# Gate columns z, the gate and the state-space part of the output projection: a move ahead of and into the third attention pattern

## The chip, the core and the metric

One of the eight cores of a Trainium2 chip runs the whole layer. The metric is the device time of one execution in microseconds; a set of runs is told by its median. The core's engines are TensorE (PE in the rows, its weight loads PEld), VectorE (DVE), ScalarE (ACT), GpSimd (POOL) and SyncE (SP), whose only work here is to issue DMAs. The order of the instructions on each engine is fixed when the program is built, and each engine, SyncE's queue of DMAs too, goes through its own in that order.

## What is computed

A one-layer decoder trunk over 1024 prompt rows and 8 decode rows, T = 1032 columns in the kernel (activations lie transposed: features on partitions, rows as columns). The mixer, cut to what matters:

```
qkv, z, xbc, dt = split(rmsnorm(x) @ w_in)
for g in 3 patterns:                         # windows 128, 512, 2048; dilations 1, 4, 16
    o[g], lse[g] = dilated_window(rope(q[g]), rope(k[g]), v[g])
attn = sum(softmax(lse over g)[g] * o[g])    # "merge", (.., 512)
y    = ssd_chunked(conv(xbc), dt)            # (.., 1024)
ssm  = rmsnorm((y + d_skip * xs) * silu(z), ssd_norm_w)
mix  = concat(attn, ssm) @ w_out
x    = x + rmsnorm(mix); x = x + rmsnorm(swiglu(rmsnorm(x)))
```

The decode rows attend over caches of past keys and values with the same weights.

## The kernel before

All is float32. Operands of the large products are split into two exact parts (`xh`, `xl` for the input; `wh`, `wl` for a weight tile), and a product is the sum of three: xh·wh, xh·wl, xl·wh. `load_w` loads a 128x1024 weight tile (L141) and GpSimd splits it (L156, L158). `unit` (L169) multiplies one tile with one of three chunks of 344 columns: 8 steps of 128 by 3 parts, 24 matmuls. `gemm` does so for its chunks, and `scaled` (L239) evicts each from PSUM by VectorE, times the row scale.

A scheduler of the Tile framework sets each engine's order by priority: the kinds are "evac", "w" (weights), "side", "late" and "main", in falling rank. The large matmuls are "main" and stand in the order in which the program is written; attention, gate and merge steps go in between where their inputs come.

The stages in the order of the program: xBC columns, convolution and state-space scan (its output goes to DRAM, `y_d`); `pattern(0)`, `pattern(1)`, `pattern(2)`, each with four head pairs; per pair `do_v`, `do_qk` twice (rotation: ScalarE L614, GpSimd L615, VectorE L619) and `attend`, eight blocks of scores, softmax and values (L645 to L687), whose result goes to `n_d` (L689). `dec_scores(g)` (L747 to L754) follows each pattern: keys of the caches times a broadcast query (GpSimd L748, VectorE L749). Behind `pattern(2)` come the rest of the decode scores, then:

- the merge, of "late" rank: the three patterns' statistics come back from DRAM (`sn`, L818), give weights (`w_d`, L844); then 16 steps, four quarters of 256 columns by four head pairs, each: load of three patterns' rows `nt` (L849) and of the weights `wt` (L852), GpSimd multiply (L854), VectorE adds (L855, L856), ScalarE cast to `ah` (L857), VectorE rest to `al` (L858). The pool `mgp` holds two `nt` and two `wt`.
- the values of the caches, "late" too: 24 loads `cvt` (L870) through five buffers, GpSimd and VectorE multiplies (L873), VectorE adds (L876, L877), a matmul (L878) each for eight rows.
- z columns and gate, 8 gemms: eviction to `zt` (L239), load of `y_d` (L907), silu (L909), multiply to `yg` (L910), squares (L913, L915), their sum `acc` on GpSimd (L917); then the norm's weights split the gated rows into `sh` and `sl` (L923, L924), in buffers that held `xh` and `xl`; and `rt`, the row scale (L192).
- state-space part of the output projection: chunks 0 and 1 of eight output tiles, 48 matmuls each, into `mix`; the first two tiles side by side, step by step as `sh` and `sl` come (L954).
- attention part: `load_pair` (L976 to L979) casts on ScalarE and splits on GpSimd, `unit` with `ah` and `al` (12 matmuls a chunk), added to `mix` (L1010); chunk 2 of the state-space part stands between; norms, and SwiGLU.

## Time and profile before

| | us |
|---|---|
| median of 3 runs (lowest, highest) | 1947.85 (1947.51, 1948.57) |
| span of the profiled execution | 1955.3 |
| TensorE busy in it | 1827.1 (93%) |
| VectorE busy | 1071.0 (55%) |
| GpSimd busy | 856.4 (44%) |
| ScalarE busy | 549.2 (28%) |

The times of single instructions come from the profiled execution, whose span is the figure that they add up to. TensorE is busy for 93% of it, but the share is an average over stages; of the 40 slices of the span the ones from the 21st on, behind the third pattern, fall to 7 and 8 tenths, and the granted clock falls to 8 tenths there.

### The profile page before, as it was taken

The numbers are of one execution on the slowest core, as the hardware profiler recorded it, in microseconds if no ns is written. First come the engines' busy times: TensorE is split into PE (matmuls) and PEld (weight loads), VectorE is DVE, ScalarE is ACT, GpSimd is POOL, SyncE is SP. The second block draws the span as 40 slices with busy tenths as digits, with TensorE's granted clock in tenths as the row PEclk, the third lists the DMA queues.
The fourth block names the chain that finished last, engine by engine and source line by source line (L and its number), as shares of the span: only waits on it lengthen the run. The fifth ranks groups of instructions, "written<-read, shape, count | busy, mean of one in ns | idle before, by whom it ended". The sixth has DMA issues, their size and how long they took to land.

```text
span 1955.3 us, 29265 instructions
## 1 busy us (share of the span) xinstructions
PE 1827.1 (93%) x11685; PEld 1712.4 (88%) x11685; DVE 1071.0 (55%) x1917; ACT 549.2 (28%) x1084; POOL 856.4 (44%) x557
## 2 busy tenths in 40 slices
PE   7999989999999999998789889999999999999994
PEld 7998777888887898886678879999999999999993
DVE  7866776768774554556884796330233223321348
ACT  5322344343533344452231334111111001100142
POOL 6332356665435534356755564223223332233325
PEclk9999999999999999999889999999999999999997
DMA  5322333443324433365554444236533753355362
GB/s 188 114 92 87 111 110 100 126 127 110 117 83 153 161 99 104 130 233 150 154 158 130 134 134 151 97 128 244 178 108 103 253 172 119 119 202 196 116 251 87
DMA packets 125545, 275.27 MB, mean 141 GB/s; under 512 B 17616, under 2 KB 83632, under 8 KB 124000
## 3 DMA queue, kind: packets, MB, share of 16 engines
q1 hardware_dynamic: 125408, 273.39, 42.8%
q8 instruction: 92, 1.51, 0.3%
q14 instruction: 45, 0.37, 0.1%
HBM read 235.86 MB, written 125.47 MB: 185 GB/s over the span
## 4 chain that ended last, share of the span: by engine, by line
PE 39%; DVE 7%; DMA 2%; issue 1%; POOL 1%; ACT 1%; DVEq 0%; SPq 0%; POOLq 0%; ACTq 0%
PE g L169 14%; PE pu L169 12%; PE pg L169 12%; DMA nt<-n_d 1%; DVE mix L1030 1%; DVE fl L1033 1%; PE g L954 1%; DVE nt L856 1%; DVE nt L855 1%; DMA xr<-in_xT 0%; DVE mix L1029 0%; POOL nt L854 0%; DVE fr L192 0%; DVE nr L192 0%; DVE sl L924 0%
## 5 line engine op out<-in xcount | busy, mean ns | idle before, releaser
L169 PE MATMUL g<-xh,wh 128*128 128x344 f32 x1344 | 446.0, 332 | 32.4 <-DVE rw L239 12.7
L169 PE MATMUL g<-xl,wh 128*128 128x344 f32 x1344 | 443.2, 330 | 2.8 <-DVE xl L218 2.7
L169 PE MATMUL g<-xh,wl 128*128 128x344 f32 x1344 | 441.9, 329 | 1.9 <-POOL wl L158 1.2
L156 POOL TENSOR_SCALAR wh<-wr 128x1024 fp32r<-128x1024 f32 (+1 forms) x133 | 140.4, 1056 | 674.5 <-PE g L169 355.8
L158 POOL TENSOR_TENSOR wl<-wr,wh 128x1024 fp32r<-128x1024 f32 (+1 forms) x133 | 312.8, 2352 | 9.8
L169 PEld LDWEIGHTS g<-xh,wh 128*128 128x128 f32 x1344 | 258.1, 192 | 46.4 <-issue 14.4
L169 PEld LDWEIGHTS g<-xh,wl 128*128 128x128 f32 x1344 | 258.1, 192 | 11.5 <-issue 7.5
L169 PEld LDWEIGHTS g<-xl,wh 128*128 128x128 f32 x1344 | 258.0, 192 | 11.0 <-issue 6.1
L239 DVE TENSOR_TENSOR u<-pu,rf 128x344 f32<-128x344 f32 x66 | 34.0, 515 | 237.5 <-PE pu L169 237.5
L169 PE MATMUL pg<-fh,wh 128*128 128x344 f32 x504 | 158.8, 323 | 4.9 <-DVE mix L1010 4.9
L169 PE MATMUL pg<-fl,wh 128*128 128x344 f32 x504 | 162.1, 322 | 0.0
L169 PE MATMUL pu<-fl,wh 128*128 128x344 f32 x504 | 161.8, 321 | 0.0
L169 PE MATMUL pg<-fh,wl 128*128 128x344 f32 x504 | 161.4, 320 | 0.0
L169 PE MATMUL pu<-fh,wh 128*128 128x344 f32 x504 | 161.0, 319 | 0.0
L169 PE MATMUL pu<-fh,wl 128*128 128x344 f32 x504 | 160.4, 318 | 0.0
L169 PE MATMUL g<-hl,wh 128*128 128x344 f32 x432 | 137.8, 319 | 0.0
L169 PE MATMUL g<-hh,wl 128*128 128x344 f32 x432 | 137.4, 318 | 0.0
L169 PE MATMUL g<-hh,wh 128*128 128x344 f32 x432 | 137.1, 320 | 0.0
L659 ACT ACTIVATE sm<-sm,ngm 128x128 f32<-128x128 f32 (+1 forms) x192 | 84.9, 443 | 183.5 <-DVE ngm L655 177.2
L1088 ACT CAST hh<-s 128x344 fp32r<-128x344 f32 x66 | 31.7, 480 | 296.6 <-DVE s L1087 296.6
L614 ACT COPY sw<-rw 32x1032 f32<-32x1032 f32 x96 | 101.0, 1052 | 30.5 <-DVE rw L239 29.4
L1085 ACT ACTIVATE s<-s 128x344 f32<-128x344 f32 x66 | 32.5, 492 | 247.6 <-DVE s L239 247.4
(325 smaller groups left out, 3815.9 us busy)
## 6 DMA issues: line engine op xcount, KB each, us to landing
out_skv<-in_cache SPq DMA_DIRECT2D x64, 1023.5 KB, 5.4
wr<-in_w_in SPq DMA_DIRECT2D x56, 512.0 KB, 3.7
wr<-in_w_fin SPq DMA_DIRECT2D x44, 512.0 KB, 3.6
out_skv<-in_cache SPq DMA_DIRECT2D x16, 1022.0 KB, 5.4
wr<-in_w_out SPq DMA_DIRECT2D x24, 512.0 KB, 4.7
wr<-in_w_fout SPq DMA_DIRECT2D x24, 384.0 KB, 3.9
e<-cs_d SPq DMA_DIRECT2D x16, 512.0 KB, 4.1
n_d<-nh SPq DMA_DIRECT2D x12, 512.0 KB, 3.6
```

The source lines that it names most:

```text
L156: nc.gpsimd.tensor_scalar(out=wh[:, :cols], in0=wr[:, :cols], scalar1=1.0, scalar2=0.0, op0=ALU.mult, op1=ALU.add)
L158: nc.gpsimd.tensor_tensor(out=wl[:, :cols], in0=wr[:, :cols], in1=wh[:, :cols], op=ALU.subtract)
L169: nc.tensor.matmul(ps, x[:, ws], y[:, c0:c1], start=(k == 0 and j == 0), stop=(k == n - 1 and j == 2))
L239: return nc.vector.tensor_tensor(out=dst, in0=ps, in1=r[:dst.shape[0], c0:c1], op=ALU.mult)
L614: nc.scalar.copy(sw[q * 32:(q + 1) * 32, 0:T], rw[s * 32:(s + 1) * 32, :])
L659: nc.scalar.activation(out=sm[:, h, :nk], in_=sm[:, h, :nk], func=AF.Exp, scale=SCALE, bias=ngm[:, g, j, i:i + 1], accum_out=den[:, g, j, ...
L855: nc.vector.tensor_tensor(out=nt[:, 0], in0=nt[:, 0], in1=nt[:, 1], op=ALU.add)
L856: nc.vector.tensor_tensor(out=nt[:, 0], in0=nt[:, 0], in1=nt[:, 2], op=ALU.add)
L954: nc.tensor.matmul(pq[m][c], ws[m][j == 1][:, k * P:(k + 1) * P], (sl if j == 2 else sh)[k][:, CH[c][0]:CH[c][1]], start=(k == 0 and j == ...
L1030: nc.vector.scalar_tensor_tensor(out=mv, in0=mv, scalar=nw(MIX_POST, m), in1=x[:, m % 2], op0=ALU.mult, op1=ALU.add)
L1085: last = nc.scalar.activation(out=s, in_=s, func=AF.Silu)
L1088: nc.scalar.copy(hh[:, c0:c1], s)
```

## The change

The loop over the z columns, the gate, the sum of squares and the row scale `rt` stand between `dec_scores(1)` and `pattern(2)`. The gate's steps have rank "side", not "evac"; the gated rows go to DRAM (`yg_d`), and are loaded again behind the decode scores (a pool of four buffers), split into `sh` and `sl`. The loop of the state-space part has one output tile side by side with the arrival of `sh` and `sl` and not two, over the pool of two PSUM banks alone; `psa` joins the pools behind it and not ahead of it. Nothing of the products, the merge or the cache values themselves is changed. Comments are gone, which moves line numbers: the merge's are L895 to L904, the load and split of the gated rows L841 to L845, cache values L916 to L924, the first state-space matmuls L952, the attention part's eviction L1009.

```diff
@@ ahead of the third pattern
     dec_scores(1)
+    gp = pool(gst, "gp", 2, side="left")
+    with prio("side"):
+        rt = rowp.tile([P, T], F32, tag="row", name="rt")
+        acc = gp.tile([P, T], F32, tag="acc", name="acc", bufs=1)
+    for k in range(KT):
+        zt = gp.tile([P, T], F32, tag="zt", name="zt")
...
+        gemm(a["w_in"][36 + k], 1024, xh, xl, ev)
+        with prio("side"):
+            yt = gp.tile([P, T], F32, tag="yt", name=f"yg{k}")
+            nc.sync.dma_start(out=yt, in_=y_d[k])
+            nc.scalar.activation(out=zt, in_=zt, func=AF.Silu)
+            nc.vector.tensor_tensor(out=yt, in0=yt, in1=zt, op=ALU.mult)
+            nc.sync.dma_start(out=yg_d[k], in_=yt)
...
+                    nc.gpsimd.tensor_tensor(out=acc, in0=acc, in1=zt, op=ALU.add)
...
     pattern(2)
@@ behind the decode scores
-    gp = pool(gst, "gp", 2, side="left")
+    ygp = pool(gst, "ygp", 4, side="left")
+    sh, sl = [], []
+    with prio("evac"):
+        for k in range(KT):
+            yt = ygp.tile([P, T], F32, tag="yt", name=f"yt{k}")
+            nc.sync.dma_start(out=yt, in_=yg_d[k])
...
+            nc.scalar.activation(out=hi, in_=yt, func=AF.Copy, scale=nw(SSD_NORM, k))
+            nc.vector.scalar_tensor_tensor(out=lo, in0=yt, scalar=nw(SSD_NORM, k), in1=hi, op0=ALU.mult,
+                                           op1=ALU.subtract)
@@ behind the cache values: z loop and gate taken out; state-space part
-    gpools.append(psa)
     ngp[0] = 0
-    ws = [ssm_w(m) for m in range(2)]
-    pq = [[gps() for c in range(2)] for m in range(2)]
+    w0 = load_w(a["w_out"][0][:, 512:1536], 1024)
+    pq = [gps() for c in range(2)]
...
-    for m in range(2, KT):
+    for m in range(1, KT):
         gemm(a["w_out"][m][:, 512:1536], 1024, sh, sl, ssm_ev(m), cc=(0, 1))
+    gpools.append(psa)
+    ngp[0] = 0
```

How this moves instructions shows at three places. First TensorE, at the end of the last key column of the third pattern (L169 with `xh7`, `xl7`; L679 and L666 are attention blocks of the third head pair). Before:

```order
L169 MATMUL g_8083<-xh7_119,wl_8026 128x344
L679 MATMUL nps_7774<-pt_7786,vt_7482 64x128 x2
L666 MATMUL ptp_7802<-ident_90,sm_7796 128x128 x2
L169 MATMUL g_8083<-xl7_127,wh_8025 128x344
L169 MATMUL g_8716<-xh0_112,wh_8711 128x344
L169 MATMUL g_8716<-xh0_112,wl_8712 128x344
L169 MATMUL g_8716<-xl0_120,wh_8711 128x344
L169 MATMUL g_8716<-xh1_113,wh_8711 128x344
L169 MATMUL g_8716<-xh1_113,wl_8712 128x344
```

After:

```order
L169 MATMUL g_8838<-xh7_119,wl_8781 128x344
L679 MATMUL nps_8529<-pt_8541,vt_8237 64x128 x2
L666 MATMUL ptp_8557<-ident_90,sm_8551 128x128 x2
L169 MATMUL g_8838<-xl7_127,wh_8780 128x344
L738 MATMUL rtp_9028<-ident_90,dec2_365 8x128 x4
L679 MATMUL nps_8529<-pt_8560,vt_8237 64x128 x2
L666 MATMUL ptp_8570<-ident_90,sm_8564 128x128 x2
L679 MATMUL nps_8529<-pt_8573,vt_8237 64x128 x2
L603 MATMUL vtp_8670<-ident_90,vp_8668 128x128 x4
L603 MATMUL vtp_8676<-ident_90,vp_8668 128x128 x4
L645 MATMUL sps_8876<-qr_8871,qr_8775 128x128
L645 MATMUL sps_8877<-qr_8871,qr_8775 128x128
```

In before the z columns (`xh0` with a new weight) follow at once and go on between the blocks; in the changed kernel the blocks of the last head pair, its value transposes (L603) and scores (L645) stand there with no large product between them. The first 48 matmuls of the state-space part (L952) begin 31 rows behind the first row shown, among the last blocks.

Second GpSimd, at the last merges (`nt` multiply: L854 before, L900 after; L156 and L158 split a weight tile, L919 cache values, L979 and L978 the attention part's weights). Before:

```order
L156 TENSOR_SCALAR wh_9727<-wr_9726 128x1024
L158 TENSOR_TENSOR wl_9728<-wr_9726,wh_9727 128x1024
L854 TENSOR_TENSOR nt_8553<-nt_8553,wt_8555 128x768
L854 TENSOR_TENSOR nt_8563<-nt_8563,wt_8565 128x768
L156 TENSOR_SCALAR wh_9785<-wr_9784 128x1024
L158 TENSOR_TENSOR wl_9786<-wr_9784,wh_9785 128x1024
L854 TENSOR_TENSOR nt_8573<-nt_8573,wt_8575 128x768
L854 TENSOR_TENSOR nt_8583<-nt_8583,wt_8585 128x768
L156 TENSOR_SCALAR wh_9843<-wr_9842 128x1024
L158 TENSOR_TENSOR wl_9844<-wr_9842,wh_9843 128x1024
L156 TENSOR_SCALAR wh_9901<-wr_9900 128x1024
L979 TENSOR_TENSOR wal0_9962<-wr_9963,wah0_9961 128x1024
```

After:

```order
L158 TENSOR_TENSOR wl_9930<-wr_9928,wh_9929 128x1024
L900 TENSOR_TENSOR nt_9297<-nt_9297,wt_9299 128x768
L900 TENSOR_TENSOR nt_9307<-nt_9307,wt_9309 128x768
L900 TENSOR_TENSOR nt_9317<-nt_9317,wt_9319 128x768
L900 TENSOR_TENSOR nt_9327<-nt_9327,wt_9329 128x768
L900 TENSOR_TENSOR nt_9337<-nt_9337,wt_9339 128x768
L900 TENSOR_TENSOR nt_9347<-nt_9347,wt_9349 128x768
L900 TENSOR_TENSOR nt_9357<-nt_9357,wt_9359 128x768
L900 TENSOR_TENSOR nt_9367<-nt_9367,wt_9369 128x768
L900 TENSOR_TENSOR nt_9377<-nt_9377,wt_9379 128x768
L900 TENSOR_TENSOR nt_9387<-nt_9387,wt_9389 128x768
L978 TENSOR_TENSOR wal0_9990<-wr_9991,wah0_9989 128x1024
```

In before a weight split stands between two and two multiplies to the end; in the changed kernel the last of the state-space part's splits stands ahead of the seventh multiply, and ten multiplies follow without one.

Third VectorE, at the end of the merges (L855, L856, L858 before; L901, L902, L904 after; L239 on `mix` are evictions of the state-space part; L1010 and L1009 are the first evictions of the attention part). Before:

```order
L858 TENSOR_TENSOR al_8395<-nt_8573,ah_8394 128x256
L239 TENSOR_TENSOR mix4_9490<-g_9758,rt_8707 128x344
L855 TENSOR_TENSOR nt_8583<-nt_8583 128x256
L856 TENSOR_TENSOR nt_8583<-nt_8583 128x256
L858 TENSOR_TENSOR al_8395<-nt_8583,ah_8394 128x256
L239 TENSOR_TENSOR mix5_9491<-g_9790,rt_8707 128x344
L239 TENSOR_TENSOR mix5_9491<-g_9816,rt_8707 128x344
L239 TENSOR_TENSOR mix6_9492<-g_9848,rt_8707 128x344
L239 TENSOR_TENSOR mix6_9492<-g_9874,rt_8707 128x344
L239 TENSOR_TENSOR mix7_9493<-g_9906,rt_8707 128x344
L239 TENSOR_TENSOR mix7_9493<-g_9932,rt_8707 128x344
L1010 TENSOR_TENSOR mix0_9486<-mix0_9486,g_9991 128x344
```

After:

```order
L901 TENSOR_TENSOR nt_9377<-nt_9377 128x256
L902 TENSOR_TENSOR nt_9377<-nt_9377 128x256
L904 TENSOR_TENSOR al_9199<-nt_9377,ah_9198 128x256
L901 TENSOR_TENSOR nt_9387<-nt_9387 128x256
L902 TENSOR_TENSOR nt_9387<-nt_9387 128x256
L904 TENSOR_TENSOR al_9199<-nt_9387,ah_9198 128x256
L1009 TENSOR_TENSOR mix0_9514<-mix0_9514,g_10019 128x344
L1009 TENSOR_TENSOR mix1_9515<-mix1_9515,g_10034 128x344
```

In before six evictions of the state-space part stand behind the last merge, and one ahead of it; in the changed kernel all of them stand ahead of these rows, and the attention part follows the last merge directly.

## Rows read from the trace of the kernel before

**Rows 1.** The page's first line.

```profile
span 1955.3 us, 29265 instructions
```

**Rows 2.** Timeline of TensorE: start us, us, engine, line, operation, out<-in, shapes, count.

```profile
834.55 0.40 PE L169 MATMUL g<-xh,wh 128*128 128x344 f32 x1
...
1068.74 0.32 PE L169 MATMUL g<-ah,wah 128*128 128x344 f32 x1
```

**Rows 3.** Windows: stretch, us, busy PE, PEld, DVE, ACT, POOL, clock, DMA, GB/s.

```profile
560.00:680.00 120.00, 111.99 (x755) 97.57 (x753) 69.99 (x161) 44.74 (x100) 62.26 (x38) 0.96 0.43 137
834.00:896.00 62.00, 57.30 (x388) 50.68 (x387) 38.54 (x92) 30.17 (x60) 38.91 (x22) 1.00 0.60 198
896.00:932.00 36.00, 27.84 (x131) 19.69 (x130) 23.68 (x36) 7.64 (x10) 18.85 (x13) 0.91 0.57 162
932.00:1051.00 119.00, 95.45 (x504) 87.36 (x504) 93.55 (x94) 25.66 (x37) 76.86 (x41) 0.87 0.53 152
```

**Rows 4.** Chain of waits, in order of time: start us, us, what.

```profile
1033.27 1.85 POOL nt L854
...
1036.43 2.48 DVE nt L856
...
1039.88 4.26 DMA nt<-n_d
...
1044.31 1.85 POOL nt L854
...
1049.87 20.17 PE g L169 x111
...
1213.95 3.76 PE pg L169 x24
```

**Rows 5.** Timeline of GpSimd, columns as in rows 2, idle time and releaser last.

```profile
932.12 2.00 POOL L854 TENSOR_TENSOR nt<-nt,wt 128x768 f32<-128x768 f32 x1 [2.92 <-DMA wt<-w_d]
...
937.37 2.84 POOL L917 TENSOR_TENSOR acc<-acc,zt 128x1032 f32<-128x1032 f32 x1
...
1041.36 1.84 POOL L854 TENSOR_TENSOR nt<-nt,wt 128x768 f32<-128x768 f32 x1 [2.74 <-DMA nt<-n_d]
...
1054.85 2.41 POOL L979 TENSOR_TENSOR wal<-wr,wah 128x1024 fp32r<-128x1024 f32 x1 [3.85 <-ACT wah L978]
```

**Rows 6.** Timeline of VectorE.

```profile
844.33 3.07 DVE L619 TENSOR_TENSOR qr<-rw,sw 128x1024 f32<-128x1024 f32 x1 [1.72 <-POOL sw L615]
...
937.88 2.60 DVE L855 TENSOR_TENSOR nt<-nt 128x256 f32<-128x256 f32 x1
...
1050.62 0.65 DVE L858 TENSOR_TENSOR al<-nt,ah 128x256 fp32r<-128x256 f32 x1 [0.53 <-ACT ah L857]
```

**Rows 7.** Waits from 834 to 1068: who waited for whom, us, times, longest.

```profile
PE g L169 <- DVE zt L239: 12.2, 4, 5.4
...
SPq L141 <- POOL wl L158: 13.4, 4, 8.2
```

**Rows 8.** Tile yg, the eight loads of y_d.

```profile
DMA to landing us min/median/max: 7.5/7.6/8.5
```

**Rows 9.** Timeline of SyncE, the last head pair's store.

```profile
896.89 0.33 SPq L689 DMA_DIRECT2D n_d<-nh  x1
```

**Rows 10.** Tile nt: operation, count, ns least/median/most, first and last start.

```profile
L854 POOL TENSOR_TENSOR nt<-nt,wt x16: 1807/1862/2266, 932.1 to 1044.3; 128x768 f32<-128x768 f32 x16
L855 DVE TENSOR_TENSOR nt<-nt x16: 361/1038/2621, 937.9 to 1046.8; 128x256 f32<-128x256 f32 x16
...
DMA to landing us min/median/max: 3.5/4.4/7.5
```

**Rows 11.** Groups of VectorE, 932 to 1051: busy us, mean ns, idle before.

```profile
L924 DVE SCALAR_TENSOR_TENSOR sl<-yg,par,sh 128x1032 fp32r<-128x1032 f32 x8 | 13.8, 1743 | 0.4 <-ACT sh L923 0.4
...
L910 DVE TENSOR_TENSOR yg<-yg,zt 128x1032 f32<-128x1032 f32 x4 | 7.3, 1824 | 2.2 <-ACT zt L909 2.2
```

More of the change, by code (lines that the diff above doesn't have):

```diff
@@ L762, in trunk, with ev @@
         dec_scores(1)
+    gst = ExitStack()
+    gp = pool(gst, "gp", 2, side="left")
[4 more added lines that the diff above has]
+        zt = gp.tile([P, T], F32, tag="zt", name="zt")
+        def ev(c, ps, zt=zt):
+            c0, c1 = CH[c]
+            return scaled(zt[:, c0:c1], ps, c, rin)
+        gemm(a["w_in"][36 + k], 1024, xh, xl, ev)
[5 more added lines that the diff above has]
+            nc.sync.dma_start(out=yg_d[k], in_=yt)
+            if k == 0:
+                nc.scalar.activation(out=acc, in_=yt, func=AF.Square)
+            else:
+                nc.scalar.activation(out=zt, in_=yt, func=AF.Square)
+                if k < KT - 1:
+                    nc.gpsimd.tensor_tensor(out=acc, in0=acc, in1=zt, op=ALU.add)
+    with prio("side"):
+        for c, (c0, c1) in enumerate(CH):
+            sp_ = side_ps("ztp")
+            nc.tensor.matmul(sp_[:, :CW], ones, acc[:, c0:c1], start=True, stop=False)
+            nc.tensor.matmul(sp_[:, :CW], ones, zt[:, c0:c1], start=False, stop=True)
+            rms(sp_[:, :CW], rt[:, c0:c1])
+    gst.close()
     pace[0] = RATE[0]
@@ L802, in trunk @@
     gst = ExitStack()
-    gp = pool(gst, "gp", 2, side="left")
+    ygp = pool(gst, "ygp", 4, side="left")
[4 more added lines that the diff above has]
+            nc.sync.dma_start(out=yt, in_=yg_d[k])
+            hi = actp.tile([P, T], F32R, tag="act", name=f"sh{k}")
+            lo = actp.tile([P, T], F32R, tag="act", name=f"sl{k}")
+            nc.scalar.activation(out=hi, in_=yt, func=AF.Copy, scale=nw(SSD_NORM, k))
+            nc.vector.scalar_tensor_tensor(out=lo, in0=yt, scalar=nw(SSD_NORM, k), in1=hi, op0=ALU.mult,
+                                           op1=ALU.subtract)
+            sh.append(hi)
+            sl.append(lo)
+    gst.close()
     right = ExitStack()
@@ L890, in trunk @@
     rst.close()
-    with prio("side"):
-        rt = rowp.tile([P, T], F32, tag="row", name="rt")
-        acc = gp.tile([P, T], F32, tag="acc", name="acc", bufs=1)
-    yg = []
-    for k in range(KT):
-        zt = gp.tile([P, T], F32, tag="zt", name="zt")
-        def ev(c, ps, zt=zt):
-            c0, c1 = CH[c]
-            return scaled(zt[:, c0:c1], ps, c, rin)
-        gemm(a["w_in"][36 + k], 1024, xh, xl, ev)
-        with prio("side"):
-            yt = mixp.tile([P, T], F32, tag="mix", name=f"yg{k}")
-            nc.sync.dma_start(out=yt, in_=y_d[k])
-        with prio("evac"):
-            nc.scalar.activation(out=zt, in_=zt, func=AF.Silu)
-            nc.vector.tensor_tensor(out=yt, in0=yt, in1=zt, op=ALU.mult)
-            yg.append(yt)
-            if k == 0:
-                nc.scalar.activation(out=acc, in_=yt, func=AF.Square)
-            else:
-                nc.scalar.activation(out=zt, in_=yt, func=AF.Square)
-                if k < KT - 1:
-                    nc.gpsimd.tensor_tensor(out=acc, in0=acc, in1=zt, op=ALU.add)
-    sh, sl = [], []
-    with prio("evac"):
-        for k in range(KT):
-            hi = actp.tile([P, T], F32R, tag="act", name=f"sh{k}")
-            lo = actp.tile([P, T], F32R, tag="act", name=f"sl{k}")
-            nc.scalar.activation(out=hi, in_=yg[k], func=AF.Copy, scale=nw(SSD_NORM, k))
-            nc.vector.scalar_tensor_tensor(out=lo, in0=yg[k], scalar=nw(SSD_NORM, k), in1=hi, op0=ALU.mult,
-                                           op1=ALU.subtract)
-            sh.append(hi)
-            sl.append(lo)
-        for c, (c0, c1) in enumerate(CH):
-            sp_ = att_ps("ptp")
-            nc.tensor.matmul(sp_[:, :CW], ones, acc[:, c0:c1], start=True, stop=False)
-            nc.tensor.matmul(sp_[:, :CW], ones, zt[:, c0:c1], start=False, stop=True)
-            rms(sp_[:, :CW], rt[:, c0:c1])
-    gst.close()
-    gpools.append(psa)
-    ngp[0] = 0
     np_ = pool(mst, "np", 2, side="left")
@@ L942, in ssm_ev @@
         return lambda c, ps: scaled(mix[m][:, CH[c][0]:CH[c][1]], ps, c, rt)
-    def ssm_w(m, share=False):
-        return load_w(a["w_out"][m][:, 512:1536], 1024, share)
-    ws = [ssm_w(m) for m in range(2)]
-    pq = [[gps() for c in range(2)] for m in range(2)]
+    ngp[0] = 0
+    w0 = load_w(a["w_out"][0][:, 512:1536], 1024)
+    pq = [gps() for c in range(2)]
     with prio("main"):
         for k in range(KT):
-            for m in range(2):
-                for j in range(3):
-                    for c in range(2):
-                        nc.tensor.matmul(pq[m][c], ws[m][j == 1][:, k * P:(k + 1) * P],
-                                         (sl if j == 2 else sh)[k][:, CH[c][0]:CH[c][1]],
-                                         start=(k == 0 and j == 0), stop=(k == KT - 1 and j == 2))
+            for j in range(3):
+                for c in range(2):
+                    nc.tensor.matmul(pq[c], w0[j == 1][:, k * P:(k + 1) * P],
+                                     (sl if j == 2 else sh)[k][:, CH[c][0]:CH[c][1]],
+                                     start=(k == 0 and j == 0), stop=(k == KT - 1 and j == 2))
     with prio("evac"):
-        for m in range(2):
-            for c in range(2):
-                ssm_ev(m)(c, pq[m][c])
-    for m in range(2, KT):
+        for c in range(2):
+            ssm_ev(0)(c, pq[c])
+    for m in range(1, KT):
         gemm(a["w_out"][m][:, 512:1536], 1024, sh, sl, ssm_ev(m), cc=(0, 1))
+    gpools.append(psa)
+    ngp[0] = 0
     ahs = [ah[:, k] for k in range(HP)]
```

## The prediction

> **What bounds the kernel now.** I read, in this order, the page's first line, TensorE's timeline at the two ends of the stage that the change touches, the busy time by stage, the chain of waits through that stage, and the operations on its critical tile.
>
> The profiled execution lasts 1955.3 us [rows 1], 7.45 us (0.4%) above the median of the runs, 1947.85. I work out a difference on the trace and carry it to the median unchanged.
>
> Call T0 the moment when TensorE has no product of a query, key or value column left: 834.55, when the first z product starts [rows 2]. The first attention-part matmul of the output projection starts at 1068.74 [rows 2]. The tail between them is **234.2 us** long, and the change replaces it. Up to 1051, TensorE is busy for 57.30 of 62, 27.84 of 36 and 95.45 of 119 us of it [rows 3]: it stands still for 4.7 + 8.2 + 23.6 = 36.5 us. In the last 119 us the granted clock is 0.87 on average, that is 1.2 GHz for a part and 2.4 for the rest, so products there also run slower than elsewhere. In a stretch where nothing is late, 24 matmuls take 3.76 us [rows 4], 0.157 each. The 576 z matmuls are worth 90.3 us at that rate, and the 384 state-space ones of chunks 0 and 1 60.2.
>
> The chain of waits shows what holds the tail: from 1033 on it runs through the merge of the patterns, and TensorE has it again only from 1049.87 [rows 4]. One step of the merge is a load (4.26 us), a multiply on GpSimd (1.85), two adds on VectorE (2.48 for a slow one), a cast, a subtraction, and its buffer (one of two) goes to the next load [rows 4]. The 16 merges begin at 932.12 [rows 5], T0 + 97.6, and the last subtraction ends at 1051.27 [rows 6]. In before, z and state-space products fill TensorE beneath them.
>
> **The change part by part.**
>
> *z products ahead of the third pattern.* All 576 move ahead of T0. TensorE has work in hand there: it is busy 111.99 of 120 us in a stretch of the third pattern [rows 3]. So T0 moves later by their price, 90.3 us. The 8.0 idle us of such a stretch bound what more work at hand could fill; the 12.2 us for which z products waited for their evictions [rows 7] bound what they could lose, now that their gate steps stand at a lower rank. I take 0 and keep −8 and +12. The break-even tail of the changed kernel is 234.2 − 90.3 = **143.9 us**.
>
> *The gate.* Eight VectorE multiplies, GpSimd adds and ScalarE steps move too. Ahead of the third pattern they lie beside products, and nothing there reads their result; VectorE and GpSimd are busy 69.99 and 62.26 of 120 us [rows 3]. Cost 0; without that cover six GpSimd adds of 2.84 us [rows 5], 17.0, would lie bare, which the slow rival's size takes in. The eight stores and loads of the gated rows are new, and no row shows them; a load of the same size lands in 7.5 to 8.5 us [rows 8]. Four buffers let four run together, under the last head's attention; at most one landing, 8.5, if they are not hidden.
>
> *The tail of the last head.* In before its rotated key is ready at 847.40, T0 + 12.9 (the 3.07 us add at 844.33 [rows 6]); its result is stored at 896.89 [rows 9], T0 + 62.3. So the eight blocks take 49.5 us, between z products. In the changed kernel they follow each other on TensorE almost alone, but their VectorE and ScalarE steps and the decode scores stay: 37 us is my estimate, between nothing gained (49.5) and 31, at which about a third of it had been waiting behind z products. Result stored at T0 + 50 (44 to 62).
>
> *To the first merge.* From that store to the first multiply takes 35.2 us in before (932.12 − 896.89). Between them lie a load of the statistics, the store of the weights and their load, three landings of 4.4 [rows 10], so 13 us at the least, and queue places behind loads of cache values, which remain. I take 25 (18 to 35): first merge at T0 + 75 (68 to 88).
>
> *The merges.* With two buffers the period of a pair counts. In before it is (1041.36 − 932.12) / 7 = 15.6 us on average [rows 5], and 1044.31 − 1033.27 = 11.0 at the end [rows 4], where one weight split stands in each pair. From their stretch the change takes four gate multiplies (7.3 us) and eight lower parts sl (13.8) of VectorE [rows 11], some 2.6 us a pair, and five of eight weight splits. In the changed kernel three splits, and GpSimd's multiplies for four of the eight cache rows, stand among the first six merges and neither among the last ten, as its order shows. I take 14 for each of the first three periods, between 11.0 and 15.6, and 10.5 for four more, a little under the best; from the last pair's first multiply to the end 1051.27 − 1041.36 = 9.9. Sum 42 + 42 + 9.9 = **93.9 us**. By the fastest that I find likely (three at 12, four at 9.9) it is 85.5, at the old pace 15.6 x 7 + 9.9 = 119.1.
>
> *Behind the merges.* In before six state-space evictions stand behind the last merge, and TensorE has products; now nothing is left for it. The first attention product waits for the last merge, then a weight cast and split, of which the split takes 2.41 us [rows 5]; the cast shows no row here, and I take 1.1, under half the split, together 3.5 us.
>
> *State-space products.* 48 start inside the last head's blocks, 336 follow: 336 x 0.157 = 52.8 us from about T0 + 50, all before the merges end at T0 + 169. They hide, and so does the single weight load in place of two. Queue places remain: SyncE's order now puts the fourth and fifth weight tiles of this part ahead of the merge's loads, and each waits for GpSimd to finish an earlier tile, with all later loads behind it. Such a wait was 8.2 us at its longest in before [rows 7]; I take 2, between 0 and 8.
>
> Sum: 75 + 93.9 + 3.5 + 2 = 174.4, minus 143.9 = **+30 us, 1978**. At the low ends, 68 + 85.5 + 3.5 − 143.9 = +13 (1961); at the high ends, 88 + 119.1 + 3.5 − 143.9 = +67 (2015).
>
> *A rule weighed.* An add of the merge takes 0.361 us at the least, 1.038 in the median [rows 10]; the one at 937.88 took 2.60 [rows 6], begun while a GpSimd add of 2.84 us that started at 937.37 was under way [rows 5], and it ended 0.27 us behind that. The Trainium skill, "SBUF — State Buffer", section "Who interferes with whom", says that a VectorE instruction with two SBUF inputs and a GpSimd instruction that reads SBUF take turns at a shared port pair, the second blocking till the first ends. The trace agrees here. By that rule alone the adds behind the last weight split would fall towards their least, and my sum by an estimated 8 us.
>
> **The rivals.**
>
> *Faster: the merges run at latency alone.* With no gate, no lower parts and few splits beside them, one buffer's cycle would be a landing of 3.5, a multiply of 1.81 and four short steps at 0.361 [rows 10], 6.75 us for a pair. Eight pairs take 54.0; with the first merge at T0 + 68 the tail is 68 + 54.0 + 3.5 = 125.5, so −18: **1929**. TensorE's own work would allow it (T0 + 103). It decides from a pair of (143.9 − 3.5 − 75) / 8 = 8.2 us, or 9.1 with the early start. For it speaks the bare last ten multiplies in GpSimd's order; against it, that the best pair of before, with one split beside it, took 11.0. Chance 0.11.
>
> *Same.* Pairs of some 8.5 us with the start at 75, or the 8 us gain ahead of T0 together with the low ends: 1944 to 1952, centre **1948**. Chance 0.06.
>
> *Slower still: merges keep their old pace and start.* If SyncE's queue places set them and not VectorE, 97.6 + 119.1 + 3.5 = 220.2, +76: **2024**. For it: the cycle of two buffers remains, and GpSimd's multiplies still stand behind cache values. Against it: 21.1 us less VectorE work beside them. Chance 0.08.
>
> *That the change does not do what it says:* if the state-space products do not start inside the last head's blocks, 48 matmuls (7.5 us) come later and still hide; no time of its own.
>
> **How the numbers follow.** Forecast 0.75, at 1978, its own range 1961 to 2015. This kernel's measurement can tell about 0.2%, 3.9 us, from no change. Faster 0.11, same 0.06, slower 0.75 + 0.08 = 0.83. The range for 8 in 10 reaches down to the lower edge of the same case, 1944, and up to 2010; it leaves out the faster rival and the old pace.
>
> **What the changed profile would show.** Right: T0 about 90 us later; TensorE idle for over 60 us between T0 and the first attention product, most of it behind the last state-space matmul; the chain of waits through the merge's loads, multiplies and adds for over 90 us; the first merge near T0 + 75, pairs of 10 to 14. Wrong: a tail under 144 us; TensorE busy up to the first attention product; pairs under 8.2; or T0 later by more than 102 us, which would put the loss ahead of the third pattern.

## The result

The changed kernel is slower. Its runs have a median of 1997.34 us (1992.57 to 1999.65, four runs) beside 1948.21 for the kernel before, and the measured ratio is **1.0235**, 95% interval 1.0219 to 1.0252: some 46 us. The forecast was +30, 1978, with a range of 1944 to 2010. Times below are such ratios on 1948 us: 1994 for the changed kernel.

The profiled execution of the changed kernel, from its page (compare [rows 1]):

```profile
span 1997.9 us, 29309 instructions
PE 1828.0 (91%) x11685; PEld 1710.4 (86%) x11685; DVE 1066.3 (53%) x1917; ACT 551.7 (28%) x1086; POOL 850.1 (43%) x557
```

The span is 42.6 us longer, and the engines have hardly more to do: TensorE is busy for 1828.0 us against 1827.1, ScalarE for 2.5 us more, VectorE and GpSimd for less. The loss is idle time. TensorE's timeline at the two ends of the tail, as [rows 2]; the last two columns are the idle time ahead and what ended it:

```profile
933.50 0.40 PE L169 MATMUL g<-xl,wh 128*128 128x344 f32 x1
933.74 0.60 PE L738 MATMUL rtp<-ident,dec 128*8 128x128 f32 x4
...
1107.64 1.84 PE L169 MATMUL g<-ah,wah 128*128 128x344 f32 x4 [40.19 <-ACT wah L977]
...
1110.59 0.49 PE L169 MATMUL g<-al,wah 128*128 128x344 f32 x1
```

The tail now goes from 933.74 to 1107.64, 173.9 us, and TensorE has stood still for 40.19 us when the attention part begins. Busy time by stage, columns as in [rows 3], shows where in the tail the idle time lies:

```profile
600.00:655.00 55.00, 49.80 (x331) 43.13 (x332) 26.50 (x73) 20.95 (x47) 25.22 (x17) 0.94 0.39 133
655.00:700.00 45.00, 39.83 (x250) 34.89 (x249) 26.52 (x61) 18.81 (x40) 22.53 (x12) 0.92 0.47 159
700.00:933.80 233.80, 233.80 (x1541) 217.19 (x1540) 110.90 (x235) 84.43 (x168) 92.04 (x46) 1.00 0.36 120
933.80:982.00 48.20, 29.84 (x168) 20.50 (x166) 31.20 (x85) 26.08 (x57) 18.09 (x12) 0.68 0.62 194
982.00:1011.50 29.50, 27.27 (x156) 23.56 (x157) 23.53 (x35) 1.34 (x5) 21.12 (x14) 1.00 0.76 218
1011.50:1060.00 48.50, 34.33 (x158) 26.58 (x157) 34.74 (x40) 3.06 (x8) 34.19 (x21) 0.86 0.76 207
1060.00:1107.60 47.60, 7.45 (x49) 6.95 (x47) 20.67 (x34) 5.12 (x13) 16.55 (x9) 0.63 0.57 150
```

In the last four rows TensorE is idle for 18.4, 2.2, 14.2 and 40.2 us, 74.9 together, against 36.5 in the tail of before [rows 3]. The first of them is the last head pair's attention with little beside it, the last two are the merges. The first two rows are the end of the second pattern and the start of the z columns: 10.4 us idle.

GpSimd's timeline of the merges, as [rows 5], here with the two multiplies of a pair in one row at the end:

```profile
1011.55 2.26 POOL L900 TENSOR_TENSOR nt<-nt,wt 128x768 f32<-128x768 f32 x1
...
1024.63 1.84 POOL L900 TENSOR_TENSOR nt<-nt,wt 128x768 f32<-128x768 f32 x1 [1.30 <-DMA nt<-n_d]
...
1042.16 1.80 POOL L900 TENSOR_TENSOR nt<-nt,wt 128x768 f32<-128x768 f32 x1
...
1055.60 2.05 POOL L900 TENSOR_TENSOR nt<-nt,wt 128x768 f32<-128x768 f32 x1 [2.46 <-DVE cvt L922]
...
1070.35 3.56 POOL L900 TENSOR_TENSOR nt<-nt,wt 128x768 f32<-128x768 f32 x2 [8.25 <-DMA nt<-n_d]
1080.20 3.56 POOL L900 TENSOR_TENSOR nt<-nt,wt 128x768 f32<-128x768 f32 x2 [6.30 <-DMA nt<-n_d]
1090.03 3.92 POOL L900 TENSOR_TENSOR nt<-nt,wt 128x768 f32<-128x768 f32 x2 [6.27 <-DMA nt<-n_d]
1099.52 3.92 POOL L900 TENSOR_TENSOR nt<-nt,wt 128x768 f32<-128x768 f32 x2 [5.58 <-DMA nt<-n_d]
```

The pairs begin 13.1, 17.5, 13.4, 14.8, 9.9, 9.8 and 9.5 us apart. From 1060 on GpSimd does nothing but wait for a load and multiply twice. The chain of waits of the same stretch, as [rows 4], is one such cycle after the other (here the one from 1085, with pieces under 0.1 us left out):

```profile
1085.48 4.39 DMA nt<-n_d
...
1090.03 1.81 POOL nt L900
...
1091.86 0.44 DVE nt L901
...
1092.32 1.92 DVE nt L902
...
1094.32 0.41 ACT ah L903
...
1094.75 0.42 DVE al L904
```

Load, multiply, two adds, cast and subtraction make 9.39 us, and 9.73 lie between the start of this load and the next.

### The profile page after: what moved, and what is told of

The parts are those of the page before. It is cut to its first block, busy times and chain, and to the rows that moved or that the text cites. A ratio compares the mean times of both kernels' runs of the same rounds, so it can differ in the third digit from the quotient of the medians.

```text
span 1997.9 us, 29309 instructions
## 1 busy us (share of the span) xinstructions
PE 1828.0 (91%) x11685; PEld 1710.4 (86%) x11685; DVE 1066.3 (53%) x1917; ACT 551.7 (28%) x1086; POOL 850.1 (43%) x557
## 5 line engine op out<-in xcount | busy, mean ns | idle before, releaser
L169 PE MATMUL g<-xh,wh 128*128 128x344 f32 x1344 | 442.7, 330 | 15.3 <-DVE rw L239 7.9
L156 POOL TENSOR_SCALAR wh<-wr 128x1024 fp32r<-128x1024 f32 (+1 forms) x133 | 138.0, 1037 | 723.9 <-PE g L169 386.3
L169 PE MATMUL g<-xl,wh 128*128 128x344 f32 x1344 | 440.9, 328 | 1.9 <-DVE xl L218 1.8
L169 PE MATMUL g<-xh,wl 128*128 128x344 f32 x1344 | 439.5, 327 | 1.2 <-POOL wl L148 0.7
L158 POOL TENSOR_TENSOR wl<-wr,wh 128x1024 fp32r<-128x1024 f32 (+1 forms) x133 | 311.9, 2345 | 10.0
L169 PEld LDWEIGHTS g<-xh,wh 128*128 128x128 f32 x1344 | 256.8, 191 | 23.2 <-issue 9.7
L169 PEld LDWEIGHTS g<-xl,wh 128*128 128x128 f32 x1344 | 256.4, 191 | 9.6 <-issue 5.7
L169 PEld LDWEIGHTS g<-xh,wl 128*128 128x128 f32 x1344 | 256.1, 191 | 8.2 <-issue 5.3
L169 PE MATMUL pg<-fh,wh 128*128 128x344 f32 x504 | 158.6, 322 | 4.9 <-DVE mix L1009 4.9
L169 PE MATMUL pg<-fl,wh 128*128 128x344 f32 x504 | 161.9, 321 | 0.0
L169 PE MATMUL pu<-fl,wh 128*128 128x344 f32 x504 | 161.8, 321 | 0.0
L169 PE MATMUL pg<-fh,wl 128*128 128x344 f32 x504 | 161.3, 320 | 0.0
L169 PE MATMUL pu<-fh,wh 128*128 128x344 f32 x504 | 161.0, 319 | 0.0
L239 DVE TENSOR_TENSOR u<-pu,rf 128x344 f32<-128x344 f32 x66 | 34.0, 515 | 237.5 <-PE pu L169 237.5
L169 PE MATMUL pu<-fh,wl 128*128 128x344 f32 x504 | 160.4, 318 | 0.0
L169 PE MATMUL g<-hl,wh 128*128 128x344 f32 x432 | 137.8, 319 | 0.0
L169 PE MATMUL g<-hh,wl 128*128 128x344 f32 x432 | 137.4, 318 | 0.0
L169 PE MATMUL g<-hh,wh 128*128 128x344 f32 x432 | 137.1, 320 | 0.0
```

Of the source, the lines that this page charges most:

```text
L156: nc.gpsimd.tensor_scalar(out=wh[:, :cols], in0=wr[:, :cols], scalar1=1.0, scalar2=0.0, op0=ALU.mult, op1=ALU.add)
L158: nc.gpsimd.tensor_tensor(out=wl[:, :cols], in0=wr[:, :cols], in1=wh[:, :cols], op=ALU.subtract)
L169: nc.tensor.matmul(ps, x[:, ws], y[:, c0:c1], start=(k == 0 and j == 0), stop=(k == n - 1 and j == 2))
L239: return nc.vector.tensor_tensor(out=dst, in0=ps, in1=r[:dst.shape[0], c0:c1], op=ALU.mult)
```

## The experiments

The theory that they test: the z columns filled TensorE beside a chain that TensorE doesn't shorten (the last head pair's attention, the statistics, 16 merges), and with them gone this chain lies bare. Rivals: the loss arises ahead of the third pattern, by rank or by clock; the engines' work or SyncE's order, not the two-buffer latency, sets the merges.

**The merges taken out.** In both kernels only the first of 16 steps loads, multiplies and adds; the 16 casts and subtractions read its tile.

```diff
-                nt = mgp.tile([P, NG, QT], F32, tag="nt", name="nt")
...
+                if q == 0 and hp == 0:
+                    nt = mgp.tile([P, NG, QT], F32, tag="nt", name="nt")
...
```

> The changed kernel with 15 of the 16 merge steps left out (their loads, GpSimd multiply and two adds; the 16 casts and subtractions stay and all read the one merged tile). My theory: the stretch behind the third pattern ends with the merges, so without them it falls from 173.9 us to what TensorE's own state-space products and the last head's attention need, 110 to 125, and the kernel takes 50 to 60 us less than the changed one: 1935 to 1945. Rival, the loss lies in the z products ahead of the third pattern or in the clock: under 25 us less, above 1969.

> The kernel before with the same 15 merge steps left out. My theory: TensorE stands still for 36.5 us of its stretch, 23.6 of them beside the merges; without them 15 to 32 us less than before, 1916 to 1933, and below the changed kernel without merges by 10 to 20, since in the changed one the last head's attention has little to run beside. Rival, TensorE bounds the stretch of the kernel before anyway: under 8 us less.

The changed kernel without merges: ratio 0.9970 (0.9956 to 0.9985), 1942 us, 52 less than with them. Its first attention product starts at 1056.3, 124.5 us behind the last key column's eviction at 931.8; with merges it is 173.5 (1107.6 and 934.1). So the merges set the end of that tail. The kernel before without merges: 0.9874 (0.9853 to 0.9896), 1923 us, 25 less. The rows that these starts come from (tile ah, the changed kernel first):

```profile
L169 PE MATMUL g<-ah,wah x48: 313/320/428, 1056.3 to 1136.5; 128*128 128x344 f32 x48
L169 PE MATMUL g<-ah,wah x48: 313/320/427, 1036.4 to 1123.0; 128*128 128x344 f32 x48
```

Both came out as the theory said, and so did the order of the two: even with no merges the moved version is 19 us slower. So 27 of the 46 us are the merges', which cost 52 in the one kernel and 25 in the other, and 19 are not. Without merges TensorE is idle for 18.8 of the first 49 us behind the last key column in the moved version (931 to 980), and for 4.5 of the first 62 in the other (835 to 897). That is the last head pair's attention lying bare; that it makes up these 19 us is read from the rows, and no run tests it.

**Four merge buffers in the changed kernel.**

```diff
-    mgp = pool(rst, "mgp", 2, side="right")
+    mgp = pool(rst, "mgp", 4, side="right")
```

> The changed kernel with four buffers for the merge's loads in place of two, nothing left out. My theory, latency of a two-buffer cycle (9.8 us for each of the last pairs): with four in flight the last eight merges run at 5 to 7 us a pair, and the first eight, which stand beside cache values and weight splits, change little: 12 to 20 us less than the changed kernel, 1974 to 1982. Rival, SyncE's order or the engines' own work sets the pace: 0 to 5 us less.

1.0135 (1.0110 to 1.0159), 1974 us, 20 less than the changed kernel, the upper end of what I expected, but not by the way that I expected. The 16 multiplies now go from 1008.6 to 1078.3 and not from 1011.5 to 1101.4. GpSimd's timeline of this run has the first multiply of each pair at

```profile
1008.63 2.03 POOL L900 TENSOR_TENSOR nt<-nt,wt 128x768 f32<-128x768 f32 x1 [0.40 <-DMA wt<-w_d]
...
1015.24 1.83 POOL L900 TENSOR_TENSOR nt<-nt,wt 128x768 f32<-128x768 f32 x1 [1.96 <-DMA wt<-w_d]
...
1023.65 2.25 POOL L900 TENSOR_TENSOR nt<-nt,wt 128x768 f32<-128x768 f32 x1
...
1031.58 2.01 POOL L900 TENSOR_TENSOR nt<-nt,wt 128x768 f32<-128x768 f32 x1
...
1045.07 4.05 POOL L900 TENSOR_TENSOR nt<-nt,wt 128x768 f32<-128x768 f32 x2 [0.89 <-DMA nt<-n_d]
...
1052.81 2.03 POOL L900 TENSOR_TENSOR nt<-nt,wt 128x768 f32<-128x768 f32 x1
...
1063.82 1.83 POOL L900 TENSOR_TENSOR nt<-nt,wt 128x768 f32<-128x768 f32 x1 [2.94 <-DVE nt L902]
...
1075.97 4.12 POOL L900 TENSOR_TENSOR nt<-nt,wt 128x768 f32<-128x768 f32 x2 [0.79 <-DMA nt<-n_d]
```

The first four pairs take 36.4 us and not 58.8; the last four are no faster than with two buffers (they begin 7.7, 11.0 and 12.2 us apart), where I had expected 5 to 7 a pair. With four buffers the merges run ahead among the cache values, and GpSimd's cache values stand between the merges to the end, where in the changed kernel the last ten multiplies stand alone. The wait for a load is nearly gone (5.6 us in all for 32.8), so the cycle of two buffers no longer holds them; what holds the pace that is left is not shown. VectorE's subtractions now run among other work (tile nt of this run, columns as in [rows 10]):

```profile
L904 DVE TENSOR_TENSOR al<-nt,ah x16: 409/1430/2570, 1012.1 to 1083.2; 128x256 fp32r<-128x256 f32 x16
```

The median subtraction takes 1.430 us, against a least of 0.409.

**Half of the z columns ahead.** Columns 0 to 3 with their gate ahead of the third pattern, the rest where the kernel before has it.

```diff
+    for k in range(NA):                       # NA = 4, ahead of pattern(2)
+        zt0 = gp0.tile([P, T], F32, tag="zt", name="zt")
...
+    with prio("side"):
+        nc.sync.dma_start(out=ac_d, in_=acc0)
...
-    for k in range(KT):
+    for k in range(NA, KT):
         zt = gp.tile([P, T], F32, tag="zt", name="zt")
```

> Between the two kernels: z columns 0 to 3 with their gate ahead of the third pattern (gated rows and the partial sum of squares by way of DRAM), z columns 4 to 7, gate and state-space part where the kernel before has them. My theory, merges hold the end: the stretch grows shorter than the 49.6 us that leave it only by what VectorE is relieved of, so 5 to 20 us slower than before, 1953 to 1968, less than half of what the whole move costs or about it. Rival, each z column moved ahead costs the same: 23 us, 1971. Rival, a part moved fills idle time ahead and costs nothing behind: 1940 to 1948.

1.0153 (1.0131 to 1.0175), 1978 us: 30 us, nearer to the linear rival and beyond it. My expectation failed. T0 moved by 44.1 us (last eviction of a key column 877.7, before 833.6), as half of the columns should. But the first merge came at 998.65, 121 us behind it, where in before it is 98.5. VectorE's timeline of that run ahead of it (line numbers are a little off those of before: L869 is the last step of the weights, L193 the gate's reciprocal, L902 and L905 cache values):

```profile
981.94 0.68 DVE L902 TENSOR_TENSOR cvt<-cvt,dpt 128x512 f32<-128x512 f32 x1
982.54 5.72 DVE L869 TENSOR_TENSOR wo<-wg,md 128x64 f32<-128x64 f32 x3
988.14 2.29 DVE L193 RECIPROCAL rt<-rt 128x344 f32<-128x344 f32 x1
```

The three steps of the weights, 64 wide, are spread over 5.72 us. What makes the weights stands in VectorE's queue among cache values, lower parts sl and reciprocals, all of which still come behind the third pattern in the half move, now with less time under z products.

**The half move with the cache values held behind the weights.**

```diff
-        nc.sync.dma_start(out=w_d.rearrange("g h (n t) -> (h n) g t", t=P), in_=wts)
+        wst = nc.sync.dma_start(out=w_d.rearrange("g h (n t) -> (h n) g t", t=P), in_=wts)
...
+                after(ld, wst)                # ld: each load of cache values
```

> The half move (z columns 0 to 3 ahead) with every load of cache values held until the store of the merge's weights has landed, by a dependency; nothing left out. In the half move the first merge multiply came 50 us behind the last attention store, while VectorE worked through sums of cache values, lower parts and reciprocals between the steps of the weights. My theory: with the cache values behind, the first merge comes 15 to 25 us earlier, the end of the stretch 8 to 20 us earlier: 1960 to 1974. Rival, the merges only take longer by what was moved among them: 1978 to 1985, no change.

1.0107 (1.0088 to 1.0126), 1969 us. The first merge came at 976.84, 21.8 us earlier, although the last key column's eviction came 5.5 later in this run (883.2), and the first attention product at 1080.9 for 1090.8, 9.9 earlier: about half of the earlier start came back in longer merges. So the late start of the merges was a queue's doing, as the theory said for this run; the half move stays slower than before.

**The changed kernel without cache values** (one decode row of eight kept).

```diff
-        for b in range(NB):
+        for b in range(1):
```

> The changed kernel with the sums of cache values of seven of the eight decode rows left out (loads, multiplies, adds, matmuls). My theory: the first three pair periods of the merges (13.1, 17.5, 13.4 us) stand at that length for the cache values and the weight splits beside them; without cache values they fall to 10 to 12, and the first merge comes 3 to 8 us earlier: 12 to 25 us less than the changed kernel, 1969 to 1982. Rival, the merge's own latency sets all periods: under 5 us less.

1.0149 (1.0131 to 1.0167), 1977 us, 17 less. The first merge comes at 1002.91, the pair periods are 10.2, 11.2, 11.4, 10.4, 9.6, 9.7 and 10.6, and the tail is 154.2 us for 173.5. So the 13 to 17 us of the first three pairs were due to the cache values beside them, and about 10 is what two buffers give.

**The gate at its old rank.**

```diff
             nc.sync.dma_start(out=yt, in_=y_d[k])
+        with prio("evac"):
             nc.scalar.activation(out=zt, in_=zt, func=AF.Silu)
...
```

> The changed kernel with the gate's steps ahead of the third pattern at the rank that they have in the kernel before (evictions' rank), nothing else. T0 moved by 99.2 us with the change where 576 matmuls at full pace are 90.3. My theory: 2.7 of the rest are the six matmuls of the norm that moved along, some 5 are idle time of TensorE between the end of the second pattern and the z columns, and the gate's rank has little in it: within 3 us of the changed kernel, 1991 to 1997. Rival, the lower rank holds up the z buffers and so the products: 5 to 9 us less.

1.0261 (1.0247 to 1.0275), 1999 us: 5 us slower than the changed kernel, and not 5 to 9 faster. The traces show why: on TensorE, VectorE, ScalarE, GpSimd and SyncE the operations stand in the same order, tile for tile (buffer numbers aside), as in the changed kernel. So this rank moves nothing here, the rival by rank is out, and the run is a second measurement of the same order. Its last key eviction comes at 931.0, 3.1 earlier, and its tail is 180.3 us for 173.5: that much lies between two runs of one order, more than my bound of 3 us, and a difference of that size between two single traces shows nothing by itself.

**Three buffers in the kernel before.**

```diff
-                nt = mgp.tile([P, NG, QT], F32, tag="nt", name="nt")
+                nt = mgp.tile([P, NG, QT], F32, tag="nt", name="nt", bufs=3)
```

> The kernel before with three buffers for the merge's loads of the patterns' rows (two stay for the weights), nothing left out. My theory: GpSimd waits 29.2 us for these loads in eight of 16 steps there, and TensorE stands still for 23.6 us in the stretch of the merges; a third buffer takes a part of it: 4 to 14 us less than before, 1934 to 1944, which would be under both kernels. Rival, the two weight buffers and SyncE's order hold the cycle as before: within 3 us of before.

1.0025 (1.0015 to 1.0034): my theory failed. There is no gain, by the timing some 5 us of loss, though the one profiled execution is 2.4 us shorter than that of before. The rows show that the rival named the wrong reason too. The merges did get faster: the last subtraction starts at 1035.9 and not at 1050.6. But the attention part could not use it (tile ah of this run):

```profile
L169 PE MATMUL g<-ah,wah x48: 314/320/427, 1058.7 to 1146.9; 128*128 128x344 f32 x48
...
L858 DVE TENSOR_TENSOR al<-nt,ah x16: 411/426/2398, 934.1 to 1035.9; 128x256 fp32r<-128x256 f32 x16
```

TensorE still had state-space products until 1058.7 (1060.1 in before). In the kernel before the merges lie in the chain of waits, but TensorE's own products end later than they do. The 25 us that this kernel saved without any merges are no contradiction: there TensorE's idle time between the last key column and the attention part fell from 36.5 to 22.1 us, and the granted clock was 1.00 in the last 66 us of it, where before has 0.87 over 119 [rows 3]. I read from this that the merges cost this kernel by the work that they put into the queues beside the products, and not by when they end.

**Chunk 2 of the state-space part ahead of the attention part.** A test of the theory from the other side: give TensorE other work beside the bare chain.

```diff
+    ps2 = gps()
+    unit(ps2, w0, sh, sl, 2)
...
-        gemm(a["w_out"][m][:, 512:1536], 1024, sh, sl, ssm_ev(m), cc=(0, 1))
+        gemm(a["w_out"][m][:, 512:1536], 1024, sh, sl, ssm_ev(m))
...
-        if c == 2:
-            for m in range(KT):
-                gemm(a["w_out"][m][:, 512:1536], 1024, sh, sl, ssm_ev(m), cc=(2,), share=True)
```

> The changed kernel with chunk 2 of the state-space part (192 matmuls, 30.1 us at 0.157) done with chunks 0 and 1, ahead of the attention part, and not between its chunks 1 and 2; the second load and split of these weight tiles goes. Nothing left out. My theory: TensorE is idle for some 40 us beside the last merges, so these products run there without moving the first attention product by more than 5 us, and the stretch between it and SwiGLU (100.3 us in the changed kernel) shrinks by 15 to 28, less than 30.1 since its norms lose a cover: 10 to 25 less than the changed kernel, 1969 to 1984. Rival, VectorE, with eight more evictions beside the merges, is the bound and the merges grow by what is moved: within 5 us of the changed kernel.

> The same move of chunk 2 in the kernel before. My theory: there TensorE has products beside the merges, and its 36.5 idle us are short waits, so the 30.1 us come later by most of their length while the norms lose a cover: 5 us less to 10 us more than before, 1943 to 1958. Rival, the merges bound that stretch of the kernel before as they do in the changed one: the products fill idle time and 10 to 25 us go, 1923 to 1938.

In the changed kernel 1.0096 (1.0068 to 1.0123), 1967 us, 27 less, a little more than expected. TensorE in the stretch of the last merges (windows of this run):

```profile
1060.00:1107.00 47.00, 34.47 (x197) 33.36 (x196) 22.36 (x34) 3.44 (x9) 21.69 (x12) 0.92 0.67 163
```

It is busy for 34.47 of 47 us, where it was 7.45 of 47.60. The first attention product comes at 1114.4, only 6.8 us later for 30.1 us of products; the stretch from there to SwiGLU falls from 100.3 to 53.8 us, by 46.5 where I expected 15 to 28, and behind that 13 us come back (the span ends 803.1 us behind the first product of SwiGLU, 789.9 in the changed kernel).

In the kernel before the same move gives 0.9996 (0.9982 to 1.0009): nothing, as expected. There the first attention product comes 22.1 us later than 1068.74 (tile ah):

```profile
L169 PE MATMUL g<-ah,wah x48: 315/320/427, 1090.8 to 1131.8; 128*128 128x344 f32 x48
```

The stretch behind it falls by about as much as in the changed kernel (from 96.9 to 52.2 us), and 14 us come back behind the start of SwiGLU (803.7 for 789.6). On the trace 8.6 us are left, but the profiled execution of before was 7.1 us above its median. What differs is the idle time: up to 1051 it stays at 35.6 us, for 36.5. There the tail had no idle stretch to fill.

**Both in the changed kernel.** Chunk 2 ahead and four buffers.

> The changed kernel with both chunk 2 ahead and four merge buffers; nothing left out. My theory: with four buffers the idle time beside the merges is some 17 us (its stretch is 23 us shorter), so of chunk 2 about half is free: 25 to 40 us less than the changed kernel in all, 1954 to 1969, not under the kernel before. Rival, both gains add up in full: 1948 or less.

1.0044 (1.0027 to 1.0062), 1957 us, 37 less than the changed kernel, as expected; still 9 above before.

**Cache values behind the late merges**, with both of these.

```diff
+                after(ld, muls[min(15, HOLD + 2 * b)])   # HOLD = 8; muls: the merge's multiplies
```

> The changed kernel with chunk 2 ahead and four merge buffers, as in the run before, and every load of cache values held by a dependency until a late merge multiply (the ninth for the first decode row, two further for each row after it, the last for the rest); nothing left out. My theory: VectorE and GpSimd are the bound of the merges once four buffers hide the loads, so with cache values taken from the first eight merges and put beside the last ones and the attention part's first chunk, the merges start 4 to 8 us earlier and end 8 to 18 us earlier: 6 to 14 us less than with chunk 2 and four buffers alone, 1943 to 1951, about the kernel before or just under it. Rival, what is put behind comes back where the attention part's evictions and norms need VectorE: within 4 us of that kernel, 1953 to 1961.

1.0096 (1.0075 to 1.0117), 1967 us: 10 slower than without, where I expected 6 to 14 faster. The first half of the expectation held: the multiplies go from 999.36 to 1057.38 and not from 1005.81 to 1073.7. But the first attention product comes at 1098.0, as in the run before (1098.8). TensorE waited for VectorE's evictions (waits of this run, 933 to 1180: total, times, longest):

```profile
PE g L170 <- DVE mix L240: 19.6, 9, 5.0
```

It was 12.0 us without the hold. In neither of the two do the merges end the stretch: the last subtraction starts at 1084.1 without the hold and at 1067.1 with it, and without it TensorE is all but fully busy with its own products at the end (windows of that run):

```profile
1080.00:1100.00 20.00, 19.60 (x121) 18.51 (x122) 8.51 (x18) 5.75 (x9) 7.24 (x3) 1.00 0.49 141
```

So an earlier end of the merges by itself had nothing to give there, as in the kernel before. What was put behind came back: SwiGLU starts at 1157.9 for 1151.0, and the cast of the decode rows, whose sums the cache values feed, moved from 1088.4 to 1121.1. That VectorE as a whole is the bound then is my reading, and no run shows it. None of the versions that leave nothing out is faster than the kernel before.

## Why the prediction was right, and where it was off

The terms, on the trace:

| step | forecast, us | measured, us |
|---|---|---|
| T0 later by the z columns | 90.3 | 99.2 (834.55 to 933.74) |
| T0 to the last attention store | 50 | 48.6 (982.34) |
| T0 to the first merge | 75 | 77.8 (1011.55) |
| 16 merges | 93.9 | 94.9 (to 1106.43) |
| from there to the attention part | 3.5 | 1.2 |
| queue waits on SyncE | 2 | in the above (2.3 at the fifth pair) |
| tail | 174.4 | 173.9 |
| attention part and norms | 0 | +3.4 (100.3 for 96.9) |
| SwiGLU and the rest | 0 | +0.3 |
| sum of the change | +30 | +42.6 |

The 2.3 of the queue waits are a load for the fifth pair, issued at 1064.67, 2.3 us after its buffer was free (the subtraction begun at 1060.29 took 2.09), behind two loads of the block's input (L1026) that stood ahead of it in SyncE's queue.

The mechanism held: merges that wait for a late start, slow pairs beside cache values, then pairs of about 10, with TensorE idle beside them. That the tail came out within a microsecond is luck, since its terms miss by 2 to 3 us each and cancel. The start came 2.8 us late; the first three pairs took 44.0 us for 42 (14.7 on average), the next four 44.0 for 42 (11.0, the first of them still 14.8); the end took 6.9 for 9.9, and the way to the attention part 1.2 for 3.5. The experiments bear the causes out: without cache values the early periods fall to 10 to 11.4, without merges the tail ends after 124.5 us. For the late pairs there are the chain of waits and these even periods without cache values; four buffers shortened the early pairs and not the late ones. One sign failed: the chain of waits runs through the merges for the last 43 us, from 1064.67 on, and not for over 90; ahead of that it lies in the cache values' sums and the state-space products.

**The step that was mis-sized is the z columns ahead of the third pattern.** I priced 576 matmuls at full pace and took 0 for the rest, with 12 as the upper bound; the measured rest is 8.9. TensorE's idle time from 600 to T0 is 10.4 us, and 5.3 in the kernel before up to its T0 (94.69 busy of 100, then none idle), so 5.1 of it are idle time. The longest piece is one wait of the scores for the rotated key that VectorE makes (waits of TensorE from 600 to T0: total, times, longest; the changed kernel, then before):

```profile
PE sps L645 <- DVE qr L619: 9.8, 2, 7.9
PE sps L645 <- DVE qr L619: 4.7, 1, 4.7
```

The other 3.8 us fit the six matmuls of the norm's sum over the gated rows, which moved along and which I left out of the count: in the timeline of the changed kernel one pair of their instructions is

```profile
774.39 0.74 PE L792 MATMUL ztp<-acc,ones 128*128 128x344 f32 x2
774.97 0.74 PE L793 MATMUL ztp<-zt,ones 128*128 128x344 f32 x2
```

0.58 apart, 3.5 us for six. Of a step that is moved, every instruction counts. The idle time is in part spread between runs: in the seven other runs whose order is the same up to 980 that longest wait takes 4.99 to 5.84 us. The last key eviction comes at 929.4 to 934.1 in these eight, and at 831.1 to 835.0 in the four that have the order of before up to 870; the medians lie 98.6 us apart, so a rest of 8.3 stands. The rank of the gate steps is not its cause; what makes the part of it beyond the six matmuls stays open.

**The step that had no term** is the attention part, +3.4 us. The two kept weight splits lie bare behind the last merge (the first attention product needs its cast at 1107.64, its second part waits for the split), and matmuls run at 0.29 us apart from 1110.59 to 1113.46, then at 0.157: 16 matmuls take 6.1 us up to 1113.72, which at 0.157 would be 2.5.

The remaining 3 us (6.5 by the two medians, which lie 49.1 apart) lie between trace and timing: the span of before is 7.1 us above the median of its four runs, that of the changed kernel 0.6 above its own. Carrying a difference over unchanged cost that much.

**What was said wrongly of the kernel before.** The prediction read the chain of waits as proof that the merges hold its tail. Three buffers ended them 15 us earlier and nothing was gained; chunk 2 moved ahead found no idle stretch either. There TensorE's products end last and its 36.5 idle us are short waits, none over 5.4 us: some 30 of them on VectorE (12.2 for z evictions, [rows 7]; 7.9 for cache values, 5.3 for lower parts sl), 4.6 on GpSimd's weight splits. The chain got into the merges by one of these: at 1049.87 TensorE had waited 2.04 us for a weight split that stood behind two merge multiplies on GpSimd. It follows the release that came last, not the work that would have ended last. The number did not hang on this reading, since the tail of the changed kernel was built up from its own pieces. A slip of reading besides: nine attention products (1.4 us at 0.157) run in before from 1060.10 on among the last state-space ones, ahead of the one at 1068.74 which I called the first.

The rivals. *Latency alone*: the last pairs do run so, at 9.8 us, but not at 6.75. The load takes 4.39 in the cycle shown above and not the least of 3.5, the short steps 0.41 to 0.44, and 1.5 more go to one add: the two multiplies of a pair stand side by side, and one add of the four waits for the second. VectorE's timeline has it:

```profile
1072.18 2.00 DVE L901 TENSOR_TENSOR nt<-nt 128x256 f32<-128x256 f32 x1 [4.17 <-POOL nt L900]
1074.22 0.42 DVE L902 TENSOR_TENSOR nt<-nt 128x256 f32<-128x256 f32 x1
```

The first add takes 2.00 us, while GpSimd's double multiply runs from 1070.35 to 1073.91; the next takes 0.42. The Trainium skill, "SBUF — State Buffer", section "Who interferes with whom", has a VectorE instruction with two SBUF inputs block behind a GpSimd instruction that reads SBUF; the trace agrees. By that rule alone the prediction had the adds behind the last weight split fall to their least, 8 us less, a figure that it gives without its working; the merges' own multiplies kept that from coming true. Nor would TensorE's own work have allowed this rival at T0 + 103, as the prediction says: with the merges taken out the attention part still starts 124.5 us behind the last key column. *Old pace*: the half move came near it, with a first merge 121 us behind its T0 where queues fell out badly. The scheduler's order there, which nobody wrote by hand, was worth 9 us by the hold of the cache values alone.

## What to carry to other kernels

Before moving large products ahead, list what they run beside in their old place. Work that fills an engine beside a latency chain costs its full length again where it is moved to a stretch in which the engine is already busy, and the place that it leaves shrinks only to the chain: here T0 came 99.2 us later, and the tail became 60.3 shorter. A chain of waits names the last release: whether shortening it pays is told by when the other work would have ended, and an extra buffer or a filler moved in tests that in one run.

## What the runs showed of the hardware that was not expected

A 64-wide VectorE step of the merge's weights, 0.27 to 0.29 us in the kernel before, took up to 2.4 us in the half move: three of them took 5.72 us together, while weight splits and cache values ran on GpSimd. Small steps were held up beside GpSimd as long as the 256-wide adds (2.00 us). With four buffers the merge loads landed in 6.4 us in the median (4.2 to 10.0) for 4.8 (3.6 to 5.9) with two in the changed kernel. And TensorE came out of 40.19 us of standing still, in a stretch with a mean granted clock of 0.63 (1.2 GHz for most of it, 2.4 for the rest), at 0.29 us a matmul (granted clock 0.50 from 1107.6 to 1113.7), and ran at 0.157 from 1113.7 on (1.00).
